# Three small parameter loads moved to the wide stage, and the last two state-space groups squared in place behind their stores

## The chip, the cores and the metric

The kernel runs as one program on one core of a Trainium2 chip. The metric is the device time of one execution in microseconds. Five engines work side by side in a core: PE (TensorE, the matmuls; its weight loads are listed as PEld), DVE (VectorE), ACT (ScalarE), POOL (GpSimd) and SP (SyncE, which here only issues DMAs). Each engine runs its own list of instructions in order, and an instruction can wait for instructions of other engines and for the landing of DMAs. ACT issues DMAs too: all stores to device memory are issued from its list.

## The reference

One layer of a decoder trunk on a sequence of 1024 tokens with 1024 channels, all in float32:

```python
mod = silu(c) @ ada_w + ada_b;  shift, scale, gate = split(mod, 3)
h = rms_norm(x, norm_w) * (1 + scale) + shift
gm_u, gm_v, gm_z, ssm_z, xbc, dt_raw, g_a, g_b = split(h @ w_in)
y_a = spatial_gating(gelu(gm_u), gelu(gm_v), ...) * silu(gm_z)
xs, bm, cm = split(silu(causal_conv(xbc, conv_w, conv_b)))
dt = softplus(dt_raw + dt_bias);  a = -exp(a_log)
y_b = ssd_scan(xs, dt, a, bm, cm) + xs * d_skip        # 8 groups of 4 heads
y_b = rms_norm per group of (y_b * silu(ssm_z)), times ssm_norm_w
merged = sigmoid(g_a) * (y_a @ w_proj_a) + sigmoid(g_b) * (y_b @ w_proj_b)
out = rms_norm(x + gate * (merged @ w_out), final_norm_w)
```

The three vectors `dt_bias`, `a_log` and `d_skip` have 32 numbers each. For the norm of `y_b` each group needs, per token, the sum of the squares of its 256 channels.

## The kernel before

The program is one long body that writes each engine's list in the order of the code; helpers marked `pin` keep their place, and other instructions may be moved by the scheduler. `load` (line 90) issues on SP, `store` (line 93) on ACT. PE is kept fed through the whole program, and everything else is arranged around its list.

**Early stage.** The modulation `mod` is a row times the matrix `ada_w`, taken in eight steps `n`. In each step PE computes a `matvec(n)` (16 matmuls `pm<-aw`, where `aw` holds half a megabyte of `ada_w`), ACT copies the result to a row (line 262), PE turns it into columns (`pm<-ones,row`), DVE makes the scale and the shift from it (`md`, lines 275 and 276), and ACT applies them to the transposed tokens (line 300: `b11h`, `hf` and others). With these, PE multiplies the first columns of `w_in`, `w0` (`acc<-b11h,w0h` and the like, line 81, the line of the helper that records every ordinary matmul). The weights of step `n + 2` are loaded in step `n`. In step 1, behind the loads of `aw` and `w0r` for step 3, SP also loads the three small vectors, each broadcast to all 128 partitions: `dtb`, `abc` and `dsk` (30.0 us into the program). DVE copies `dsk` into the narrower tile `dskt` (line 503); `dskt` is first read by the state-space stage.

**Wide stage.** From about 100 us on PE multiplies with weights whose blocks (`av`) SP loads and ACT and DVE split in two parts (`p2v0h`, `p2v0l`: a value and its remainder). The function `small_parameters` runs here; it loads the other small vectors (`pkb`), behind the last `av` loads.

**State-space stage** (about 930 to 1156 us). The eight groups are taken in four pairs, and each pair in four steps `s` of 256 tokens, the two groups in turn. A group's state `st` goes round from step to step: PE reads it (`yn<-sl,st`), POOL multiplies it by a decay (line 1157), DVE adds the new part `sp` from PE (line 1159), and PE reads it again. Between these, PE fills its time with the projection of `y_a` (`pma`, 3 x 8 x 8 pairs of matmuls, one pair for each half of the tokens), which `draw(n)` takes from a generator, `n` items at a time; `left[0]` counts what is left. The result of a pair of steps, `yz` (two tiles of 128 x 512), is stored to `yb_d` (line 93) and squared, so that PE can sum the squares over the channels (`pq<-ones`, in `post2`) and DVE and POOL make the norm's factors of it (`ssq`, lines 1221 and 1225). For the groups 0 to 5, and the first half of groups 6 and 7, the squares are written over `yz`, some steps after the store, and wait for it to land (line 1210). The second half of the groups 6 and 7 is the last of the stage: its squares go into two other tiles `sq`, taken from the rings `ea_r` and `ym_r` or `y1_r`, right behind the store (line 1205). The ring slot matters, because the stage behind it takes its tiles from the same slots.

**Projection of y_b** (from 1156 us). The normed `y_b` is multiplied with `w_proj_b` in 56 units: eight for each of the products `p1`, `p3`, `p6`, `p5`, `p7`, `p2`, `p4`, 12 matmuls each (line 1592). For a unit of `p1`, `loads` fetches a piece of `y_b` (`yn<-yb_d`), the factors `rb<-rs_d` for each second unit, and the weights `p1r`; `operands` normalises the piece (`y_norm`, line 1530 on DVE), and splits it (`p1bh` on ACT, `p1bl` on DVE) and the weights (`p1a` on ACT and on DVE). Six units are loaded ahead (`LOAD`) and four prepared ahead. The code of the first six comes behind the `post2` of groups 6 and 7, which comes when five items of `pma` are left.

Of the kernel before, what the change touches and what calls it, by code (L numbers as in the profile page):

```python
# [8 lines left out]
F32 = mybir.dt.float32  # L9
# [7 lines left out]
P = 128  # L17
# [4 lines left out]
NG = 8  # L22
# [13 lines left out]
def hybrid_kernel(  # L36
# [52 lines left out]
    def load(dst, src):  # L89
        pin(nc.sync.dma_start(dst, src))  # L90
# [81 lines left out]
    with tc.tile_pool(name="p0", bufs=1, reuse_waits="tile") as p0:  # L172
# [278 lines left out]
        for n in range(1, KT):  # L451
            todo = prepare(n + 1) if n + 1 < KT else {}
            for at, _ in enumerate(first_products(n), 1):
                if at == 1 and n + 2 < KT:
                    load_aw(n + 2)
                    load_w0(n + 2)
                if at == 1 and n == 1:
                    load(dtb, dt_bias.to_broadcast([P, NH]))
                    load(abc, a_log.to_broadcast([P, NH]))
                    load(dsk, d_skip.to_broadcast([P, NH]))  # L460
                if at in todo:
                    todo[at]()
                if at == 2 and n < KT - 1:
                    split_w0(n + 1)
                between(n, at)
# [17 lines left out]

    def small_parameters():

        pkb = wide("pkb").rearrange("p (i q) -> p i q", q=P)
        G.memset(pkb[:, 0], 0.0)
        at = 0
        for src, n in [(conv_b, 32), (ssm_norm_w, 16), (gm_ln_w, 8), (gm_ln_b, 8)]:
            load(pkb[at : at + n, 0], src[0].rearrange("(r q) -> r q", q=P))  # L490
            at += n
        load(pkb[:, 1], conv_w[0].rearrange("k (i q) -> (k i) q", q=P))
        later(4, small_parameters2, pkb)
# [580 lines left out]
    class Group:  # L1074
# [118 lines left out]
        def post(self, q):  # L1193
# [6 lines left out]
                later(5, self.squares, yz, [yz[:, j] for j in range(2)])  # L1200
                later(17, self.post2, q, [yz[:, 0]])
            else:
                self.late = sq = [turn(r, f"sq{g}", F32) for r in (ea_r, (ym_r, y1_r)[g % 2])]
                for j in range(2):
                    pin(A.activation(sq[j], yz[:, j], AF.Square))
                G.tensor_add(sq[0], sq[0], sq[1])

        def squares(self, yz, sq):
            for j in range(2):
# [264 lines left out]
        run_tasks()  # L1474


    draw(left[0] - 5)
    for late in groups[NG - 2 :]:
        late.post2(1, late.late[:1])
    room.extend(ea_r[0] + [st_r[0][1]])  # L1480
    room.extend(tag for k in range(KT - 2) for tag in ya_tags[k])

# [200 lines left out]
    def ahead(u):  # L1683
        if u + LOAD < len(units):
            loads(u + LOAD)
        if u + LEAD < len(units):
            operands(u + LEAD)

    for u in range(LOAD):
        loads(u)  # L1690
        if u > 1:
            operands(u - 2)
    draw(left[0] + 1)
    room.extend(tag for k in (KT - 2, KT - 1) for tag in ya_tags[k])
    for tags, _ in (war_r[0], wah_r[0], wal_r[0], tha_r):
# [235 lines left out]
```

## Time and profile before

| | |
|---|---|
| median of 3 runs | 1400.12 us (1399.7 to 1400.92) |
| the profiled execution | 1404.41 us |
| its span, from the first instruction to the last | 1402.7 us |
| mean granted TensorE clock | 0.993 |
| busy: DVE, ACT, POOL | 74%, 57%, 13% of the span |
| DMA | 288.60 MB, mean 206 GB/s |

A row of the timeline gives an instruction, or several alike behind each other: its start in microseconds of the span, its length, engine, line, operation, the tile written and the tiles read, the shape, the count (x16), and in brackets how long the engine had been idle before it and what it was waiting for. A row with SPq or ACTq is the issue of a DMA. A row of the windows gives a stretch of time, then for each engine its busy time and the number of instructions, and at the end the granted clock of PE (1.00 is full, 0.50 half), the busy share of the DMA engines and the bytes that they moved per second.

### The profile page before, as it was taken

How to read it: one execution, taken by the hardware profiler on the slowest of the kernel's cores; microseconds unless marked ns; L12 is line 12 of the kernel's file. 1: busy time of each engine (PE TensorE's matmuls, PEld its weight loads, DVE VectorE, ACT ScalarE, POOL GpSimd, SP SyncE). 2: the span in 40 equal slices, each digit the busy share in tenths (PEclk: the TensorE clock that was granted, in tenths of full speed). 3: DMA queues.
4: the chain of work that ended last, by engine and by line, in shares of the span. 5: the costliest groups of instructions: out<-in, count | busy, mean ns of one | idle time of the engine just before them, and what ended most of it. 6: DMA issues, size and time to landing. Idle time of an engine off the chain costs nothing.

```text
span 1402.7 us, 20203 instructions
## 1 busy us (share of the span) xinstructions
PE 1370.8 (98%) x6951; PEld 1133.6 (81%) x6951; DVE 1041.7 (74%) x1724; ACT 800.0 (57%) x1447; POOL 189.1 (13%) x191
## 2 busy tenths in 40 slices
PE   8999999999999999999999999999999999999997
PEld 6588888888888888888888888888888877788786
DVE  4685876777778789788888885398777736859976
ACT  4664666667556566465576555677666714233443
POOL 1000000000000000000000000038868760000002
PEclk9999999999999999999999999999999999999999
DMA  8674534343435667787675764698787719978913
GB/s 265 176 234 137 151 120 121 100 126 118 130 99 148 195 196 246 229 260 210 196 218 177 234 205 139 212 362 305 270 272 266 266 65 323 346 250 298 381 63 120
DMA packets 247228, 288.60 MB, mean 206 GB/s; under 512 B 14509, under 2 KB 194133, under 8 KB 247125
## 3 DMA queue, kind: packets, MB, share of 16 engines
q1 hardware_dynamic: 173716, 203.76, 45.5%
q10 hardware_dynamic: 73408, 83.54, 17.5%
q8 instruction: 55, 0.90, 0.3%
q14 instruction: 49, 0.39, 0.1%
HBM read 199.79 MB, written 87.46 MB: 205 GB/s over the span
## 4 chain that ended last, share of the span: by engine, by line
PE 69%; DMA 11%; DVE 8%; ACT 4%; issue 3%; SPq 2%; POOL 2%; ACTq 0%; DVEq 0%; POOLq 0%
PE xz L565 6%; PE xx L565 6%; PE xg L565 5%; PE xcb L565 5%; PE xuz L565 5%; PE pma L81 3%; PE vx L954 3%; PE yx L565 3%; PE yz L565 3%; PE ycb L565 3%; PE yg L565 3%; PE ox L1775 2%; PE yuz L565 2%; SPq L90 2%; DMA yn<-yb_d 2%
## 5 line engine op out<-in xcount | busy, mean ns | idle before, releaser
L1104 POOL TENSOR_SCALAR_AFFINE_SELECT dcy<-dcy 128x1024 f32<-128x1024 f32 x32 | 35.0, 1092 | 794.6 <-DMA yl<-ya_d 748.6
L1109 ACT ACTIVATE dcy<-dcy,nacs 128x128 f32<-128x128 f32 x256 | 78.5, 388 | 14.1 <-POOL dcy L1104 13.7
L1101 ACT ACTIVATE ea<-dcy 64x512 f32<-64x512 f32 x64 | 40.1, 626 | 13.0 <-DMA dcy<-acs_d 12.5
L1189 DVE TENSOR_TENSOR ym<-yn,ea 128x512 f32<-128x512 f32 (+1 forms) x32 | 19.9, 622 | 32.8 <-PE yn L81 32.8
L81 PE MATMUL pma<-yh,wah 128*128 128x512 f32 x128 | 43.9, 424 | 0.0
L1129 DVE TENSOR_TENSOR dcy<-dcy,pc 128x1024 f32<-128x1024 f32 x32 | 38.9, 1217 | 5.0 <-PE pc L84 4.0
L81 PE MATMUL pma<-yh,wal 128*128 128x512 f32 x128 | 42.6, 414 | 0.0
L1024 ACT ACTIVATE ac<-ac 128x1024 f32<-128x1024 f32 x32 | 34.0, 1061 | 13.5 <-DVE ac L1022 13.2
L1191 POOL TENSOR_TENSOR yz<-y,sl 128x512 f32<-128x512 f32 x32 | 41.4, 1293 | 0.9
L81 PE MATMUL pma<-yl,wah 128*128 128x512 f32 x128 | 40.3, 396 | 0.0
L1530 DVE SCALAR_TENSOR_TENSOR yn<-yn,par,rb 128x512 f32<-128x512 f32 x32 | 23.8, 747 | 21.7 <-DMA yn<-yb_d 21.7
L1190 POOL TENSOR_TENSOR y<-y,ym 128x512 f32<-128x512 f32 (+1 forms) x32 | 36.5, 1142 | 14.6 <-DVE ym L1189 14.6
L81 PEld LDWEIGHTS yn<-sl,st 128*128 128x128 f32 x224 | 30.2, 191 | 8.4 <-POOL yz L1211 2.5
L81 PE MATMUL sp<-xe,bn 128*128 128x256 f32 x112 | 33.7, 418 | 3.1 <-DVE ssq L1221 1.6
L81 PE MATMUL yi<-dcy,xd 128*64 128x128 f32 x512 | 35.9, 284 | 0.7 <-DVE st L1159 0.7
L81 PE MATMUL yn<-sl,st 128*128 128x128 f32 x224 | 31.1, 276 | 5.2 <-DVE st L1159 5.2
L1790 POOL TENSOR_TENSOR r<-r,fnw 128x512 f32<-128x512 f32 x4 | 5.3, 1334 | 228.6 <-ACT junk L1788 228.6
L1022 DVE SCALAR_TENSOR_TENSOR ac<-c2x,cwt,ac 128x1023 f32<-128x1023 f32 (+2 forms) x24 | 30.7, 1280 | 6.2 <-ACT ac L1020 6.1
L1022 DVE SCALAR_TENSOR_TENSOR ac<-c2cb,cwt,ac 128x1023 f32<-128x1023 f32 (+2 forms) x24 | 30.6, 1275 | 5.6 <-ACT ac L1020 5.5
L824 ACT CAST wbb<-wbr 128x512 fp32r<-128x512 f32 x32 | 19.8, 619 | 26.1 <-DMA wb_d<-wbb 20.5
L986 ACT ACTIVATE vm<-vm,vr 128x128 f32<-128x128 f32 x64 | 25.8, 484 | 14.9 <-DMA vm<-v_d 10.3
L1157 POOL TENSOR_TENSOR st<-st,cd 128x256 f32<-128x256 f32 x48 | 32.9, 685 | 9.7 <-PE yn L81 6.3
(2974 smaller groups left out, 4385.3 us busy)
## 6 DMA issues: line engine op xcount, KB each, us to landing
sl<-s_d SPq DMA_DIRECT2D x32, 768.0 KB
s_d<-ac ACTq DMA_DIRECT2D x32, 512.0 KB
wb_d<-wbb ACTq DMA_DIRECT2D x32, 512.0 KB
dcy<-acs_d SPq DMA_DIRECT2D x32, 512.0 KB
av<-in_w_in_dram SPq DMA_DIRECT2D x36, 256.0 KB
aw<-in_ada_w_dram SPq DMA_DIRECT2D x16, 512.0 KB
wbr<-in_w_proj_b_dram SPq DMA_DIRECT2D x32, 256.0 KB
yb_d<-yz ACTq DMA_DIRECT2D x32, 256.0 KB
```

The costliest lines, as they stand in the source:

```text
L81: pin(PE.matmul(acc, l, r, start=first, stop=last))
L565: pin(PE.matmul(ps, lw[:, k * P : (k + 1) * P], r[k], start=first and n + k == 0, stop=n == 2 and k == 3, skip_group_check=not first))
L954: pin(PE.matmul(ps[pn][j], l[:, j * P : (j + 1) * P], r, start=nm in ("p1", "p5", "p2") and n + units[i][1] == 0, stop=n == 2 and k == 3, ...
L1022: V.scalar_tensor_tensor(ac[:, s:], cc[:, : S - s], conv_wt[:, 3 - s, i : i + 1], ac[:, s:], op0=ALU.mult, op1=ALU.add)
L1024: A.activation(ac, ac, AF.Silu)
L1101: A.activation(ea[hh * HD : (hh + 1) * HD], dcy.rearrange("p (j e) i l -> p e j (i l)", e=2)[hh * HD : (hh + 1) * HD, hh], AF.Exp)
L1104: G.affine_select(out=d8, in_=d8, compare_op=ALU.is_ge, fill=-1e30, base=0, pattern=[[0, 2 * HPG], [1, P]], channel_multiplier=-1)
L1109: A.activation(dcy[:, h, i, :], dcy[:, h, i, :], AF.Exp, bias=sub[:, i, h : h + 1])
L1129: V.tensor_tensor(d3, d3, pc[:, 0:256].unsqueeze(1).to_broadcast([P, HPG, 256]), op=ALU.mult)
L1157: G.tensor_mul(v3(s2), v3(self.st), fac(cd, g, s)[:, i].unsqueeze(2).to_broadcast([P, HPG, HD]))
L1190: G.tensor_add(y1[:, :, t0:], y1[:, :, t0:], m[:, :, t0:])
L1191: G.tensor_mul(yz, y1, sl[:, 4:6])
```

## The change

The loads of `dtb`, `abc` and `dsk` go from step 1 of the early stage to the head of `small_parameters`, ahead of its other loads. The second halves of groups 6 and 7 are squared in place, as the others are, as a task five steps behind the store (`late_squares`); the tiles `sq` are gone. The two calls of `post2` are taken apart: group 6's comes with eight items of `pma` left, ahead of the code that loads the first units of the projection of `y_b`; group 7's comes with three items left, inside that code, behind the loads of unit 3 and the operands of unit 1.

```diff
@@ early stage, step n, behind the first product
                 if at == 1 and n + 2 < KT:
                     load_aw(n + 2)
                     load_w0(n + 2)
-                if at == 1 and n == 1:
-                    load(dtb, dt_bias.to_broadcast([P, NH]))
-                    load(abc, a_log.to_broadcast([P, NH]))
-                    load(dsk, d_skip.to_broadcast([P, NH]))
                 if at in todo:
                     todo[at]()
...
     def small_parameters():
 
+        load(dtb, dt_bias.to_broadcast([P, NH]))
+        load(abc, a_log.to_broadcast([P, NH]))
+        load(dsk, d_skip.to_broadcast([P, NH]))
         pkb = wide("pkb").rearrange("p (i q) -> p i q", q=P)
...
@@ Group.post
             else:
-                self.late = sq = [turn(r, f"sq{g}", F32) for r in (ea_r, (ym_r, y1_r)[g % 2])]
-                for j in range(2):
-                    pin(A.activation(sq[j], yz[:, j], AF.Square))
-                G.tensor_add(sq[0], sq[0], sq[1])
+                self.late = [yz[:, j] for j in range(2)]
+                later(5, self.late_squares)
+
+        def late_squares(self):
+            sq = self.late
+            for j in range(2):
+                pin(A.activation(sq[j], sq[j], AF.Square))
+            G.tensor_add(sq[0], sq[0], sq[1])
...
-    draw(left[0] - 5)
-    for late in groups[NG - 2 :]:
-        late.post2(1, late.late[:1])
     room.extend(ea_r[0] + [st_r[0][1]])
...
+    draw(left[0] - 8)
+    groups[6].post2(1, groups[6].late[:1])
     for u in range(LOAD):
         loads(u)
         if u > 1:
             operands(u - 2)
+        if u == 3:
+            draw(left[0] - 3)
+            groups[7].post2(1, groups[7].late[:1])
     draw(left[0] + 1)
```

**DVE in the early stage, before.** The rows are in the order of DVE's list; `b22l` and `b11l` are remainders of the tokens for the first product, `md` the modulation of step 2.

```order
L304 TENSOR_TENSOR b21l_198<-hf_434,b21h_194 128x512
L223 TENSOR_TENSOR w0l_347<-w0r_345,w0h_346 128x256
L304 TENSOR_TENSOR b22l_182<-hf_434,b22h_178 128x512
L503 COPY dskt<-dsk 64x16 x2
L275 TENSOR_TENSOR md_497<-pm_466,par 128x1
L276 TENSOR_SCALAR md_497<-pm_466,par 128x1
L304 TENSOR_TENSOR b11l_159<-hf_500,b11h_155 128x512
```

**The same place with the change, and then the place in the wide stage to which the copy goes**, about 100 rows further down in DVE's list. (The same lines of code have other numbers with the change: 1 lower here and in the groups, 3 higher from `late_squares` to the end of the state-space stage.)

```order
L304 TENSOR_TENSOR b21l_198<-hf_434,b21h_194 128x512
L223 TENSOR_TENSOR w0l_347<-w0r_345,w0h_346 128x256
L304 TENSOR_TENSOR b22l_182<-hf_434,b22h_178 128x512
L275 TENSOR_TENSOR md_494<-pm_463,par 128x1
L276 TENSOR_SCALAR md_494<-pm_463,par 128x1
L304 TENSOR_TENSOR b11l_159<-hf_497,b11h_155 128x512
```

```order
L884 TENSOR_TENSOR p7v2l<-av_2_1163,p7v2h 128x512
L884 TENSOR_TENSOR p7v3l<-av_3_1190,p7v3h 128x512
L884 TENSOR_TENSOR p2v0l<-av_0_1209,p2v0h 128x512
L502 COPY dskt<-dsk 64x16 x2
L884 TENSOR_TENSOR p2v1l<-av_1_1211,p2v1h 128x512
L884 TENSOR_TENSOR p2v2l<-av_2_1230,p2v2h 128x512
```

The copy of `dsk` no longer stands ahead of `md`; it stands between two splits of the wide stage, `p2v0l` and `p2v1l`.

**DVE at the last step of group 6** (`s` = 3), before and then with the change; `xe` and `xd` are inputs of group 7's step 3, `y` the direct part of group 6's result, `st` the state that PE's next `yn` reads.

```order
L1129 TENSOR_TENSOR dcy_3_10556<-dcy_3_10556,pc_3_10795 128x1024
L1125 TENSOR_TENSOR xd_3_10804<-px_3_10794,dthq 128x512
L1125 TENSOR_TENSOR xe_3_10806<-px_3_10794,dde 128x512
L1185 TENSOR_SCALAR y_3_10838<-sl_3_10483,dskt,yi_3_10811 128x256 x2
L1159 TENSOR_TENSOR st_3_0_10822<-st_3_0_10822,sp_3_10820 128x256
```

```order
L1128 TENSOR_TENSOR dcy_3_10556<-dcy_3_10556,pc_3_10795 128x1024
L1124 TENSOR_TENSOR xd_3_10804<-px_3_10794,dthq 128x512
L1124 TENSOR_TENSOR xe_3_10806<-px_3_10794,dde 128x512
L1530 TENSOR_SCALAR yn_0_10964<-yn_0_10964,par_139,rb_0_10962 128x512
L1184 TENSOR_SCALAR y_3_10838<-sl_3_10483,dskt,yi_3_10811 128x256 x2
L1158 TENSOR_TENSOR st_3_0_10822<-st_3_0_10822,sp_3_10820 128x256
```

The `y_norm` of unit 0 of the projection of `y_b`, which stood behind the last `ssq`, stands here inside the last step of group 6, ahead of `y` and `st`.

**ACT from the last stores of groups 6 and 7 to the first operands of the projection**, before and then with the change. `yb_d_95` and `yb_d_96` are the two stores of group 6, `yb_d_97` and `yb_d_98` those of group 7.

```order
L93 DMA yb_d_95<-yz_2_10705 128x512
L93 DMA yb_d_96<-yz_2_10705 128x512
L1205 ACTIVATE sq_10847<-yz_2_10705 128x512
L1205 ACTIVATE sq_10848<-yz_2_10705 128x512
L1422 DMA mt_d_81<-tha_0_10596 128x512
L1422 DMA mt_d_81<-tha_1_10599 128x512
L93 DMA rs_d_63<-tri 8x128
L93 DMA yb_d_97<-yz_2_10786 128x512
L93 DMA yb_d_98<-yz_2_10786 128x512
L1205 ACTIVATE sq_10894<-yz_2_10786 128x512
L1205 ACTIVATE sq_10895<-yz_2_10786 128x512
L1567 COPY p1bh_10999<-yn_0_10981 128x512
```

```order
L93 DMA yb_d_95<-yz_2_10705 128x512
L93 DMA yb_d_96<-yz_2_10705 128x512
L1425 DMA mt_d_81<-tha_0_10596 128x512
L1425 DMA mt_d_81<-tha_1_10599 128x512
L93 DMA rs_d_63<-tri 8x128
L93 DMA yb_d_97<-yz_2_10786 128x512
L93 DMA yb_d_98<-yz_2_10786 128x512
L1208 ACTIVATE yz_2_10705<-yz_2_10705 128x512 x2
L1208 ACTIVATE yz_2_10786<-yz_2_10786 128x512 x2
L1567 COPY p1bh_10982<-yn_0_10964 128x512
L1572 COPY p1a_10966<-p1r_10967 128x512
```

Group 6's squares moved from behind its own store to behind group 7's, and all four squares now read and write the stored tile; the first operand copies of the projection still stand behind them. On SP the three small loads moved, and nothing else; PE's list differs in the places of the two `pq` alone. SP's list has the loads of the projection in the same order as before, but the first of them, `rb`, takes a ring slot that group 6's `sq` held before until its `pq`, and that now has been free since `ea` was last read there, in the groups' third step.

## The prediction

> **What bounds the kernel now.** The first view is part 1 of the page, the busy time of the engines.
>
> ```profile
> PE 1370.8 (98%) x6951; PEld 1133.6 (81%) x6951; DVE 1041.7 (74%) x1724; ACT 800.0 (57%) x1447; POOL 189.1 (13%) x191
> ```
>
> PE is busy for 98% of the span, so the time falls only where PE stands still or works at a lower clock. The second view is the list of PE's waits (total, times, longest).
>
> ```profile
> PE x0p L1592 <- ACT p1a L1572: 4.6, 1, 4.6
> ...
> PE acc L81 <- ACT b11h L300: 2.6, 1, 2.6
> ```
>
> The longest wait is before the projection of y_b, and another of the longest is in the early stage. The change touches what leads to both. I call them place A (early) and place B.
>
> **Place A: what the small loads hold up.** The timeline has the chain: SP, DVE, ACT, then PE, and in front the matmul that `md` needs.
>
> ```profile
> 30.50 0.43 SPq L90 DMA_DIRECT2D dsk<-in_d_skip_dram  x1
> ```
> ```profile
> 32.14 0.50 PE L81 MATMUL pm<-ones,row 128*128 128x1 f32 x4
> ```
> ```profile
> 36.28 0.35 DVE L503 COPY dskt<-dsk 64x16 f32<-64x16 f32 x2 [4.35 <-DMA dsk<-in_d_skip_dram]
> ```
> ```profile
> 37.03 0.78 ACT L300 ACTIVATE b11h<-px,md 128x512 fp32r<-128x512 f32 x1 [5.56 <-DVE md L276]
> ```
> ```profile
> 37.86 0.73 PE L81 MATMUL acc<-b11h,w0h 128*128 128x512 f32 x2 [2.60 <-ACT b11h L300]
> ```
>
> DVE waits 4.35 us for a tiny load that lands 5.4 us after its issue ended (36.28 less 30.93). The `md` behind it could have run from 32.64, when PE's `pm` ended. Without the copy `b11h` runs at about 33.0 and is ready at 33.8, and PE comes for it at 35.26 (37.86 less 2.60). So the gap goes, with 1.4 us to spare, and PE's earlier rows don't change.
>
> The gap has a second price, seen in the windows (clock is the number behind POOL's).
>
> ```profile
> 38.60:42.00 3.40, 3.40 (x22) 2.08 (x23) 3.16 (x6) 2.41 (x5) 0.00 (x0) 0.50 0.12 33
> ```
>
> Behind the gap PE works 3.4 us at about half clock, 1.7 us of work lost. To size both prices in one, I compare the starts of alternate matvecs, which enclose like work (each pair of steps holds one `pd<-hf,wd`).
>
> ```profile
> 29.66 1.07 PE L81 MATMUL pm<-aw,scz 128*32 128x256 f32 x16
> ```
> ```profile
> 45.32 1.07 PE L81 MATMUL pm<-aw,scz 128*32 128x256 f32 x16
> ...
> 57.22 1.07 PE L81 MATMUL pm<-aw,scz 128*32 128x256 f32 x16
> ```
>
> From 29.66 to 45.32 are 15.66 us, from 45.32 to 57.22 are 11.90: 3.8 us lost. Counted directly it is 2.6 of gap and 1.7 of half clock, 4.3. I take **4.0**; the bounds are 2.6 (a low clock that comes anyway) and 4.3.
>
> **Where the three loads go.** SP now issues them behind the last `av`, and the copy stands on DVE before `p2v1l`.
>
> ```profile
> 99.34 8.12 SPq L90 DMA_DIRECT2D av<-in_w_in_dram  x8
> ```
> ```profile
> 111.85 0.69 DVE L885 TENSOR_TENSOR p2v1l<-av,p2v1h 128x512 fp32r<-128x512 f32 x1 [2.03 <-ACT p2v1h L884]
> ```
> ```profile
> 130.68 0.39 PE L954 MATMUL vz<-p2v1l,b21h 128*128 128x512 f32 x1
> ```
>
> Issued from 107.5 to 108.9 at 0.43 each, and landing 5.4 us later, they hold DVE to some 114.3, 2.5 us past its due time. PE uses `p2v1l` at 130.68, so 16 us of slack lie behind it: **0**. If that cover were gone it would cost those 2.5.
>
> **Place B: the loads of the projection.** SP's waits (the DMA queue's own), then the timeline.
>
> ```profile
> SPq L90 <- PE pq L81: 38.0, 1, 38.0
> ```
> ```profile
> 1152.67 0.32 SPq L90 DMA_DIRECT2D rb<-rs_d  x1
> 1153.08 0.38 SPq L90 DMA_DIRECT2D yn<-yb_d  x1
> ```
> ```profile
> 1158.44 0.75 DVE L1530 SCALAR_TENSOR_TENSOR yn<-yn,par,rb 128x512 f32<-128x512 f32 x1 [4.75 <-DMA yn<-yb_d]
> ```
> ```profile
> 1159.30 0.62 ACT L1567 CAST p1bh<-yn 128x512 fp32r<-128x512 f32 x1 [11.88 <-DVE yn L1530]
> ```
> ```profile
> 1155.30 0.63 PE L81 MATMUL pma<-yh,wal 128*128 128x512 f32 x2
> 1160.49 0.80 PE L1592 MATMUL x0p<-p1bh,p1a 128*128 128x512 f32 x1 [4.56 <-ACT p1a L1572]
> ...
> 1165.64 0.39 PE L1592 MATMUL x0p<-p1bh,p1a 128*128 128x512 f32 x1
> ...
> 1168.41 0.47 PE L1592 MATMUL x0p<-p1bh,p1a 128*128 128x512 f32 x1
> ```
> ```profile
> 1162.00:1164.00 2.00, 2.00 (x5) 1.54 (x6) 2.00 (x4) 0.43 (x1) 0.00 (x0) 0.50 1.07 384
> ```
>
> SP stands 38 us, because `rb` takes the slot of group 6's `sq` and must wait for its `pq`. Everything for unit 0 then comes in a row, and PE, done at 1155.93, waits 4.56 us. Its first unit takes 5.15 us (1160.49 to 1165.64) at clock 0.50, the next 2.77: 2.4 more. Together **7.0** to be had.
>
> With the change `rb`'s slot is free by the third step, and SP's `yn` for unit 0 goes out at about 1130.6, when its own slot falls free with a `yn` of PE and this `st` of POOL:
>
> ```profile
> 1129.84 0.61 POOL L1157 TENSOR_TENSOR st<-st,cd 128x256 f32<-128x256 f32 x1 [1.35 <-PE yn L81]
> ```
>
> The rest follows in steps as slots fall free, from 1142 on.
>
> Three things take some of it back.
>
> First, `y_norm` of unit 0 now stands ahead of `st` on DVE.
>
> ```profile
> 1132.92 0.68 DVE L1125 TENSOR_TENSOR xe<-px,dde 128x512 f32<-128x512 f32 x1
> ...
> 1134.30 0.41 DVE L1159 TENSOR_TENSOR st<-st,sp 128x256 f32<-128x256 f32 x1
> ```
> ```profile
> 1134.72 1.05 PE L81 MATMUL yn<-sl,st 128*128 128x128 f32 x8
> ```
>
> PE reads that `st` the moment it is there (1134.71), so each delay of DVE is one of PE. Queued behind `y_norm` are `y`, `st` and `ym`. It costs 0.67 (0.75, overlapped) if the load has landed by 1133.5, 3 us after its issue; the row at 1158.44 has 5.4 for a load among many, which would make it 3.0. DMA is idle here, so I take **0.9**; bounds 0.6 and 3.0.
>
> Second, the squares wait for the stores. What a store takes to land, from ACT's rows of the stage:
>
> ```profile
> 1111.71 0.35 ACTq L93 DMA_DIRECT2D yb_d<-yz  x1
> ...
> 1112.09 0.46 ACTq L93 DMA_DIRECT2D yb_d<-yz  x1
> ...
> 1117.30 0.63 ACT L1210 ACTIVATE yz<-yz 128x512 f32<-128x512 f32 x1 [1.04 <-DMA yb_d<-yz]
> ...
> 1120.10 0.63 ACT L1210 ACTIVATE yz<-yz 128x512 f32<-128x512 f32 x1 [2.17 <-DMA yb_d<-yz]
> ...
> 1145.41 0.82 ACTq L93 DMA_DIRECT2D yb_d<-yz  x2
> ```
>
> From issue to square: 5.6 and 8.0 us, beside 1.75 MB of loads. Group 7's stores go out at 1145.41 and 1145.82. At 5.6 the last square runs at 1151.4, POOL's sum (1.29) ends at 1153.3, and PE comes to that `pq` at about 1153.5: no wait. Behind the squares on ACT stand `p1bh` and `p1a`, and behind these on DVE `p1bl` and the second part of `p1a`, about 3 us in all: ready at 1155, due at 1155.8. At 8.0 all is 2.4 later and PE waits 2.2. I take 5.6, since fewer loads run here, and **0.3**; bounds 0 and 2.2.
>
> The Trainium skill, "DMA: Bandwidth & Descriptors", section "Anatomy of one DMA — SWDGE (gpsimd) path", gives about 2.0 us fixed plus the bytes at 436 GB/s, for another path of issue. By it a 256 KB store would land in an estimated 2.6 us and this term be 0; the rows above, at more than twice that under load, decide.
>
> Third, unit 8, the first of `p3`. Its `p3bl` stood behind the `y_norm` of unit 10; now that of unit 11 stands ahead of it too.
>
> ```profile
> 1182.59 0.75 DVE L1530 SCALAR_TENSOR_TENSOR yn<-yn,par,rb 128x512 f32<-128x512 f32 x1 [2.68 <-DMA yn<-yb_d]
> 1183.25 0.68 DVE L1568 TENSOR_TENSOR p3bl<-yn,p3bh 128x512 fp32r<-128x512 f32 x1
> 1184.47 0.75 DVE L1530 SCALAR_TENSOR_TENSOR yn<-yn,par,rb 128x512 f32<-128x512 f32 x1 [0.53 <-DMA yn<-yb_d]
> ```
> ```profile
> 1184.79 0.39 PE L1592 MATMUL x3p<-p1bh,p1a 128*128 128x512 f32 x1
> ```
>
> PE ends `p1` at 1185.0. In these times `p3bl` would end at 1185.8 instead of 1183.9, 0.8 too late. The loads behind unit 8 come earlier by about as much as PE does, so I take **0.8**; bounds 0 and 2.
>
> All else in the moved code keeps its count: four squares at 0.63, two sums at 1.29 and 16 `pq` matmuls are the same before and after.
>
> **The sum.** 4.0 + 7.0 − 0.9 − 0.3 − 0.8 = 9.0 us. The profiled execution took 1404.41 (span 1402.7, 1.7 around it), 4.3 more than the median of the runs; 9.0 off it is 1395.4, and off the median 1400.12 it is **1391.1**, which is what I forecast.
>
> **The rivals.**
>
> *The wait moves to the stores.* If group 7's stores land after 8.0 us, PE waits 2.2 at `pq`, and may work at half clock behind it. For that, a wait of this size must lower the clock:
>
> ```profile
> 1124.45 2.04 PE L81 MATMUL sp<-xe,bn 128*128 128x256 f32 x4 [1.64 <-DVE ssq L1221]
> ```
> ```profile
> 1125.00:1126.00 1.00, 1.00 (x5) 0.80 (x3) 0.15 (x1) 0.00 (x0) 1.00 (x2) 0.50 0.00 0
> ```
>
> A wait of 1.64 us is followed by clock 0.50, for some 3.4 us of work as at A, so 1.7 lost. Price 2.2 + 1.7, less the 0.3 already in: 1394.7. For it speaks that five loads share the DMA with the stores; against it, that nothing else moves then.
>
> The Trainium skill, "TensorE: Matmul & The Clock Gate", section "Part 1: The HAM clock gate", puts the fall to half clock behind an idle window of about 3.4 us. By it waits of 1.64 and 2.60 would leave the clock whole, and this rival would be an estimated 1393.0. The trace disagrees with both rows (1.64 and 2.60 us, each followed by 0.50), so the price with the clock stands.
>
> *The load of unit 0 lands late in the groups' chain.* PE waits 2 to 3 us for `st`, with 1.7 of clock behind it: 2.8 to 3.8 more than forecast, about 1394.4. The idle DMA speaks against it.
>
> *Place B gains nothing,* because the `p3` stage behind it, with its loads and its DVE, starts no earlier: only A's 4.0, 1396.1. For it speak 384 GB/s in the window row above and that DVE waits there for `yn` again and again; against it, that those loads go out earlier as well.
>
> *Slower.* The `y_norm` within the groups' chain waits for a load that SP cannot issue at 1130.6, since a slot or an earlier DMA holds the queue, as it did for 38.0 us before. PE then stands for as long as the load is late, with clock 0.5 behind. A and B bring 11.0 less 1.1, so it decides from about 8 us of lateness (plus 1.7 of clock) on; at 12 it would be 1404. The freeing events at 1130.5 speak against it.
>
> *The change doesn't do what it says:* PE's gap at A was due to something else and B's loads still wait: 1400. Both chains are read step by step above, so little is left for it.
>
> **How the numbers follow.** Forecast 0.52 (its own range 1388.8 to 1393), stores 0.15, late load in the chain 0.12, B without gain 0.08, slower 0.08, nothing 0.05. The range runs from 1388.5 (4.3 + 7.0 and 0.6 taken back, with a small margin) to 1396.3, past the third rival. A measurement of this kernel can tell about 0.2%, 2.8 us: faster 0.87, within it 0.05, slower 0.08.
>
> **What would show it.** In A: no wait of PE for `b11h` and clock 1.00 from 36 to 42 us. In B: SP's `rb` long before 1152, `x0p` behind `pma` without a gap, first unit 2.8 us. Against me: a wait of PE for POOL's sum at the last `pq`, a wait for `st` over 1.5 us near 1130, a wait for `p3bl` over 1 us.

## The result, and the profile after

The changed kernel takes **1387.98 us** (median of 4 runs, 1385.46 to 1391.49), the kernel before in the same comparison 1400.52 (4 runs, 1399.7 to 1402.12). The ratio is 0.9911 with a 95% interval of 0.9887 to 0.9935: 12.5 us faster, between 9 and 16. The forecast was 1391.1, with a range that began at 1388.5; the time lies 0.5 us below it. The profiled execution took 1387.35 us with a span of 1385.6 (before: 1404.41 and 1402.7). One execution of `before_dve6` further down (1709.15 us at a mean granted clock of 0.751) ran in a slower state; it counts in that run's median and in none of the ratios.

Part 1 of the page, the busy time of the engines, now reads:

```profile
PE 1363.9 (98%) x6951; PEld 1131.5 (82%) x6951; DVE 1042.8 (75%) x1724; ACT 801.4 (58%) x1447; POOL 190.4 (14%) x191
```

The counts are those of before. PE's busy time fell by 6.9 us, though it does the same work: that work runs at full clock where it had run at about half. Some 1.7 of it, an estimate from 3.4 us at half clock, are no part of the change: in this profile of before the clock fell behind a wait for `ssq` at 1124, and in this one of after it didn't (see the last section). The rest of the gain is waits. Both long waits of before are gone from PE's list (total, times, longest):

```profile
PE yn L81 <- DVE st L1158: 4.7, 4, 2.2
...
PE sp L81 <- DVE ssq L1224: 1.6, 1, 1.6
...
PE oy L1780 <- DVE ma11h L1631: 0.3, 1, 0.3
```

**Place A.** The same alternate matvecs as before, from the timeline of PE, and then the windows where the clock had been 0.50:

```profile
28.98 1.07 PE L81 MATMUL pm<-aw,scz 128*32 128x256 f32 x16
...
40.47 1.07 PE L81 MATMUL pm<-aw,scz 128*32 128x256 f32 x16
...
52.47 1.07 PE L81 MATMUL pm<-aw,scz 128*32 128x256 f32 x16
```
```profile
36.00:40.00 4.00, 3.97 (x27) 3.19 (x24) 3.07 (x7) 2.22 (x5) 0.00 (x0) 1.00 0.71 209
40.00:44.00 4.00, 4.00 (x35) 2.64 (x34) 2.90 (x6) 3.88 (x8) 0.00 (x0) 1.00 0.63 175
```

The first pair of steps takes 11.49 us, the second 12.00: the 15.66 of before have become a pair like any other, and the clock is whole. Where the copy went, the view of the tile `dskt` shows that DVE now waits for the same load in the wide stage, and nobody waits for DVE there:

```profile
L502 DVE COPY dskt<-dsk x2: 167/169/171, 107.9 to 108.1; 64x16 f32<-64x16 f32 x2
its engine sat idle before it (us, times) until:
  DMA dsk<-in_d_skip_dram: 2.9, 1
```

**Place B.** SP's rows, then PE's around the first unit of `p1`, and the window of the stage:

```profile
1109.18 0.63 SPq L90 DMA_DIRECT2D rb<-rs_d  x1
1123.72 0.32 SPq L90 DMA_DIRECT2D yn<-yb_d  x1
```
```profile
1148.80 0.62 PE L81 MATMUL pma<-yh,wal 128*128 128x512 f32 x2
1149.26 0.40 PE L1592 MATMUL x0p<-p1bh,p1a 128*128 128x512 f32 x1
...
1152.00 0.39 PE L1592 MATMUL x0p<-p1bh,p1a 128*128 128x512 f32 x1
```
```profile
1150.00:1200.00 50.00, 50.00 (x223) 41.17 (x222) 37.85 (x62) 16.25 (x28) 2.01 (x1) 1.00 0.95 344
```

SP issues `rb` 39 us ahead of the last `pma`, and `x0p` follows that `pma` without a gap. The first unit takes 2.74 us (1152.00 less 1149.26) where it took 5.15, and PE stands for nothing in 50 us. What the other three terms of the forecast became is read further down, beside the experiments.

### The profile page after: what moved, and what is told of

The parts are those of the page before. It is cut to its first block, busy times and chain, and to the rows that moved or that the text cites. A ratio compares the mean times of both kernels' runs of the same rounds, so it can differ in the third digit from the quotient of the medians.

```text
span 1385.6 us, 20200 instructions
## 1 busy us (share of the span) xinstructions
PE 1363.9 (98%) x6951; PEld 1131.5 (82%) x6951; DVE 1042.8 (75%) x1724; ACT 801.4 (58%) x1447; POOL 190.4 (14%) x191
## 4 chain that ended last, share of the span: by engine, by line
PE 85%; DMA 6%; DVE 3%; ACT 2%; issue 2%; POOL 2%; SPq 1%; POOLq 0%; ACTq 0%; DVEq 0%
PE xz L564 6%; PE xx L564 6%; PE xcb L564 6%; PE xuz L564 6%; PE xg L564 5%; PE pma L81 4%; PE ox L1780 3%; PE ycb L564 3%; PE yp L1592 3%; PE yz L564 3%; PE vx L953 3%; PE yx L564 3%; PE yg L564 3%; PE yuz L564 3%; DMA yb_d<-yz 2%
```

## The experiments

Each run was timed against the kernel before, on the same chip as the run. A single stretch of PE's list says more than the total here, since each part of the change has its own place. The columns of the table are in microseconds, from one profiled execution each: "A" from the start of the second to the start of the last of the eight matvecs (the expectations below call it "from the first to the last"); "step" from the second last to the last `sp` of the state-space stage, the place where PE waits for `st`; "B" from the `pq` of group 7's first half (1146.16 before) to the start of unit 1 of `p1`, the second of its units; "p3, p6" from the first unit of `p3` to the first of `p5`; "last" from the first `oy`, the last product, to the end of the span.

| kernel | median | ratio, 95% interval | A | step | B | p3, p6 | last |
|---|---|---|---|---|---|---|---|
| before (first profile) | 1400.52 | | 38.95 | 4.50 | 19.48 | 44.86 | 74.90 |
| before_again | 1399.89 | 1.0008 (0.9995–1.0021) | 38.20 | 4.50 | 19.89 | 43.73 | 75.29 |
| loads_only | 1397.13 | 0.9985 (0.9971–1.0000) | 34.89 | 4.48 | 19.49 | 43.79 | 74.12 |
| copy_pinned | 1395.72 | 0.9971 (0.9959–0.9984) | 34.86 | 4.50 | 19.39 | 44.48 | 72.82 |
| before_plus8 | 1403.75 | 1.0024 (1.0011–1.0038) | 38.58 | 4.50 | 19.43 | 45.66 | 75.25 |
| before_dve6 | 1398.16 | 0.9979 (0.9966–0.9993) | 37.71 | 4.48 | 20.17 | 45.56 | 72.84 |
| apart_only | 1399.57 | 0.9992 (0.9978–1.0005) | 38.39 | 4.50 | 17.54 | 47.65 | 73.47 |
| inplace_only | 1391.48 | 0.9937 (0.9922–0.9952) | 37.11 | 4.92 | 14.35 | 43.52 | 74.99 |
| late_only | 1389.13 | 0.9934 (0.9914–0.9955) | 40.20 | 4.92 | 12.37 | 43.52 | 72.79 |
| after (first profile) | 1387.98 | 0.9911 (0.9887–0.9935) | 34.89 | 4.92 | 12.38 | 43.52 | 72.81 |
| after_again | 1387.07 | 0.9909 (0.9892–0.9926) | 34.88 | 4.93 | 12.38 | 43.52 | 72.85 |
| late_copy | 1386.71 | 0.9906 (0.9891–0.9921) | 34.86 | 4.93 | 12.38 | 43.52 | 72.86 |
| after_pinned | 1386.64 | 0.9903 (0.9888–0.9918) | 34.87 | 4.50 | 12.37 | 43.52 | 72.86 |
| after_dve3 | 1384.64 | 0.9900 (0.9872–0.9928) | 34.86 | 4.92 | 12.37 | 43.52 | 72.82 |

The stretch between A and B, 1077.6 to 1083.6 us long, scatters by 6 us with no tie to any part of the change. So the columns tell the parts apart, and the totals only bear them out.

### loads_only: only the three loads move

Before, with the first two hunks of the change and no others:

```diff
-                if at == 1 and n == 1:
-                    load(dtb, dt_bias.to_broadcast([P, NH]))
-                    load(abc, a_log.to_broadcast([P, NH]))
-                    load(dsk, d_skip.to_broadcast([P, NH]))
...
     def small_parameters():
+        load(dtb, dt_bias.to_broadcast([P, NH]))
+        load(abc, a_log.to_broadcast([P, NH]))
+        load(dsk, d_skip.to_broadcast([P, NH]))
```

> The kernel before with the three small loads moved alone. Theory of the steps: the gain of the change is the sum of what each wait gives back, read from the two traces; this part gives 4.1 us (matvec starts 4.06 earlier), so about 1396.4, with x0p still waiting some 4.6 us for p1a and the waits of the later stages (p6bl 0.6, wlt 1.4) as before. Theory of scatter: what went beyond the forecast came from half-clock stretches that set in in some executions only; this part then gives between 2.6 and 4.3 and the sum of the parts alone (with the next kernel) stays at about 9.

The run took 2.1 us less than before (interval 0 to 4). A fell to 34.89, as in the changed kernel, and the wait at B stays, as the row of PE's waits shows:

```profile
PE x0p L1591 <- ACT p1a L1571: 4.5, 1, 4.5
```

A is thus this part's alone, and it is worth 3.6 us on the table: 38.45 is the mean of the seven profiles with the copy at its old place, 34.87 that of the seven without.

### late_only: only the late part

Before, with all hunks but the first two (the squares in place as `late_squares`, the two `post2` apart and behind loads).

> The late part alone: squares in place behind the store, the two products of squares apart; the small loads stand where they stood before. Theory of the steps: 7.1 at x0p, less 0.5 for y_norm within the groups' chain, plus 1.3 at p3 to p6 and 1.4 at the last product, whose waits for DVE go because the loads of the projection are ahead: about 9.3 us, 1391. Theory of scatter: the waits behind x0p go or stay by chance, and the part gives 5 to 6.5 us, 1394 to 1395. The wait of PE for b11h (2.6 us) stays by both.

It took 9.2 us less (6 to 12). B is 12.37 and the early gap is whole, with its half clock in the windows behind it:

```profile
PE acc L81 <- ACT b11h L300: 2.6, 1, 2.6
```
```profile
36.00:42.00 6.00, 4.67 (x24) 2.65 (x25) 3.63 (x9) 3.98 (x7) 0.00 (x0) 0.56 0.32 91
```

The two parts add up within their intervals: 2.1 and 9.2 are 11.3, the whole change is worth 12.5 to 12.7.

### before_again and after_again: both kernels once more

No edit; the two were run with the two parts, on the same chip, so that all stretches have a second profile.

> The kernel before once more, for its profile: the first profiled execution took 1404.41 us, 4.3 over the median of its runs. Theory of the steps: the waits (b11h 2.6, x0p 4.6, p6bl 0.6, wlt 1.4) are there again within 0.3, and what differs is a half-clock stretch or two. Theory of scatter: the two small waits behind x0p are not there in each execution. Time by both: 1399.7 to 1402.

> The changed kernel once more: its four runs spread over 6 us (1385.46 to 1391.49). Theory of the steps: 1387 to 1389 again, ratio 0.991, and what sets the runs apart is a half-clock stretch behind one of the state-space stage's waits. Theory of scatter: the median comes nearer to 1391.

The ratios are 1.0008 and 0.9909, and most stretches repeat: B is 19.89 and 12.38, "step" 4.50 and 4.93. One doesn't: "p3, p6" of before was 44.86 and is 43.73, since the wait for `p6bl` (0.6 in the first profile) isn't there in the second; that is what the theory of scatter had said of it. What the second pair of profiles settled is that the column "last" is no scatter between the two kernels, 74.90 and 75.29 against 72.81 and 72.85, over 2 us that no term of the sum had. I come back to it under before_plus8.

### copy_pinned: the loads stay, the copy goes

Before, with DVE's copy held at the place where the code has it, in the wide stage. The loads are issued in the early stage as before.

```diff
-            V.tensor_copy(dskt[part, :], dsk.rearrange("p (i h) -> p i h", h=2)[part, :, hh])
+            pin(V.tensor_copy(dskt[part, :], dsk.rearrange("p (i h) -> p i h", h=2)[part, :, hh]))
```

> The kernel before with the small loads where they were; only DVE's copy of dsk is held at its place in the code, in the wide stage, so that it no longer stands ahead of md. Theory of the copy: the loads cost nothing by themselves, PE's gap of 2.6 us at b11h and the half clock go as with the loads moved, and from the first to the last matvec PE takes 34.9 us as there (38.2 to 40.2 in the runs with the copy in its old place): 2 to 4 us faster. Rival, that the issue and transfer of the three loads delays the loads of aw and w0 behind them: part of the gap stays, 36 us or more.

It is 4.1 us faster (2.2 to 5.7), and A is 34.86. Alternate matvecs, as before:

```profile
28.85 1.07 PE L81 MATMUL pm<-aw,scz 128*32 128x256 f32 x16
...
40.33 1.07 PE L81 MATMUL pm<-aw,scz 128*32 128x256 f32 x16
```

The pair of steps that took 15.66 us takes 11.5, as in the changed kernel. The scheduler had moved the copy from the wide stage up into the early one, and it is that copy, waiting on DVE ahead of `md`, that cost the time. The issue of the three loads on SP and their transfers cost nothing that A shows. The 4.1 us aren't A's alone: "last" is 72.82 here, for the reason found under before_plus8.

### late_copy: the late part and the pinned copy

The changed kernel with the loads back in the early stage and the copy pinned, so that only the copy's place is left of the first part.

> The late part of the change, the small loads at their old place, and DVE's copy of dsk held at its place in the wide stage. If the copy was all that the early loads cost, this is the changed kernel without its first hunk: 34.9 us from the first to the last matvec and 1386 to 1388. Rival: the loads at their old place still cost something beside the late part, 1389 or more.

It takes 1386.71, the changed kernel 1387.98 and 1387.07: nothing is missing. Moving the loads did its work by moving the copy.

### inplace_only: in place, the products not apart

Before, with `late_squares`, but both `post2` where they were, behind each other and ahead of the loads.

```diff
-                self.late = sq = [turn(r, f"sq{g}", F32) for r in (ea_r, (ym_r, y1_r)[g % 2])]
-                for j in range(2):
-                    pin(A.activation(sq[j], yz[:, j], AF.Square))
-                G.tensor_add(sq[0], sq[0], sq[1])
+                self.late = [yz[:, j] for j in range(2)]
+                later(5, self.late_squares)
...
```

(`late_squares` follows as in the change.)

> The kernel before with the squares of the last halves in place behind their stores, and both products still together with five items of pma left, ahead of the code of the loads. Theory of the slot: what held the loads of the projection was the ring slot of sq alone, so SP's first rb goes out 40 us earlier again and x0p starts without a gap; in the trace of the changed kernel the sum of group 7's squares was ready about when PE would come to its product with five items left, so PE waits 0 to 1 us there: 1389 to 1391, like the late part alone. Rival, that the products must stand apart: PE waits 2 us or more at the second product for the sum of the squares, and half clock behind it: 1393 to 1395.

The loads go out early, as in the changed kernel, and it is 8.7 us faster (6.7 to 10.9). But B is 14.35, 2.0 more than with the products apart. PE's row of the second `pq`, and the window behind it:

```profile
1148.29 1.05 PE L81 MATMUL pq<-ones,yz 128*128 128x1 f32 x8 [0.29 <-POOL yz L1210]
```
```profile
1150.00:1152.00 2.00, 2.00 (x7) 1.54 (x6) 2.00 (x7) 1.46 (x3) 1.20 (x1) 0.54 0.96 358
```

With both `pq` in a row, group 7's is reached before POOL's sum is there. The wait is only 0.29 us, yet the clock behind it is 0.54, and that is where most of the 2.0 goes. In before the same 16 matmuls stood in a row without a wait (from 1151.65 on), and the clock stayed at 1.00 from 1153 to 1156. This is the rival of the stores in small. Standing apart is worth 2.0 us, 0.3 of it the wait and the rest clock.

### apart_only: the products apart, not in place

Before, with only the two `post2` moved as in the change; `sq` still takes ring tiles.

> The kernel before with the two products apart (eight and three items left) and the squares in the ring slots as before. Theory of the slot: rb still waits for group 6's product, which now ends about 1.4 us earlier; the gap before x0p falls from 4.6 to some 3.2 us and the half clock behind it stays: 1397 to 1399. Rival, that the place of the products is what counts: 1392 to 1394.

No net change (1.1 us faster, 0.7 slower to 3.1 faster). SP's `rb`, and two rows of PE:

```profile
1146.32 0.32 SPq L90 DMA_DIRECT2D rb<-rs_d  x1
```
```profile
1153.97 0.60 PE L1589 MATMUL x0p<-p1bh,p1a 128*128 128x512 f32 x1 [3.00 <-ACT p1a L1569]
...
1191.54 0.62 PE L1589 MATMUL y0p<-p3bl,p3a 128*128 128x512 f32 x1 [2.15 <-DVE p3bl L1565]
```

`rb` still waits for the slot of group 6's `sq`, and goes out when that group's `pq` frees it, now with `pma` still to come (it was 1152.67 before). That shortens the gap at B only from 4.56 to 3.00. And what B gains, 2.1 (19.64, the mean of the six kernels without the late part, less 17.54), is lost again in `p3`: there PE waits 2.15 for `p3bl` and 47.65 stand against 44.68. So it is the squares in place that free the slot: alone they bring B from 19.64 to 14.35, 5.3 of the 7.3 us, and the products apart add the other 2.0 once the slot is free. And the third term of the forecast, a `p3bl` that comes too late, is a real mechanism; it bites here.

### after_pinned: the first y_norm held behind the groups' chain

The changed kernel with `y_norm` of unit 0 kept at its place in the code, so that DVE does `st` first.

```diff
-        V.scalar_tensor_tensor(t, t, snw[:, n : n + 1], rbs[n // 2, h], op0=ALU.mult, op1=ALU.mult)
+        keep = pin if (n, h) == (0, 0) else lambda i: i
+        keep(V.scalar_tensor_tensor(t, t, snw[:, n : n + 1], rbs[n // 2, h], op0=ALU.mult, op1=ALU.mult))
```

> The changed kernel with one instruction held at its place in the code: the y_norm of unit 0, which the scheduler had put ahead of y and st in group 6's last step, now stands behind group 6's last ssq. Theory of the steps: its 0.46 us on PE's path go, and the chain of unit 0 (y_norm, p1bh, p1bl, the second part of p1a) is ready about 1 us later than before, still ahead of PE; x0p without a gap: 0.4 us faster than the changed kernel in that stretch, too little for the clock on the wall. Rival, that the chain is too late then: a wait at x0p of 1 us or more and half clock behind it, 2 to 3 us slower than the changed kernel. DVE's list is 4 places longer ahead of the products of the last units; for that see the next run.

"Step" falls from 4.92 to 4.50 and nothing else moves; the difference in time to after_again (0.9903 against 0.9909) is inside the intervals. In the changed kernel DVE's rows are

```profile
1126.53 0.74 DVE L1530 SCALAR_TENSOR_TENSOR yn<-yn,par,rb 128x512 f32<-128x512 f32 x1
...
1127.97 0.41 DVE L1158 TENSOR_TENSOR st<-st,sp 128x256 f32<-128x256 f32 x1
```

and PE's row for that `st` is

```profile
1128.53 0.68 PE L81 MATMUL yn<-sl,st 128*128 128x128 f32 x4 [0.19 <-DVE st L1158]
```

The load of unit 0, issued at 1123.72, was there when DVE came at 1126.53, without a wait, so the term is `y_norm` alone: 0.42 us.

### before_plus8 and before_dve6: what makes the last part shorter

The column "last" fell by over 2 us in the changed kernel, behind work that the change doesn't touch. The waits of PE from 1300 on name the tile in before; in after only the 0.3 for `ma11h` is left (the row stands in its list above):

```profile
PE oy L1775 <- DVE wlt L1672: 1.4, 1, 1.4
PE oy L1775 <- DVE ma11h L1631: 0.5, 1, 0.5
```

`wlt` is prepared by DVE, and DVE was late from the stage of `p7` and `p2` on, because loads for it landed late; this link is read from the rows. SP's rows there, in before and then in after, show one issue of 2.29 us, and the like one of 0.43:

```profile
1256.67 2.29 SPq L90 DMA_DIRECT2D yn<-yb_d  x1
```
```profile
1241.60 0.43 SPq L90 DMA_DIRECT2D yn<-yb_d  x1
```

And beside it, in the view of the DMA queues over 5 us (packets, MB, share of 16 engines), stands one packet of the queue that carries instructions, first in before (1255 to 1260), then in after (1240 to 1245):

```profile
q14 instruction: 1, 0.01, 2.6%
```
```profile
q14 instruction: 1, 0.01, 0.4%
```

2.6% of 16 engines over 5 us are 2.1 us of one engine; 0.4% are 0.3. The same small packet took seven times as long in before, and SP's issue stood beside it for as long. My first thought, that loads and DVE run further ahead in the changed kernel, fell with these rows: at the start of `p7` DVE and SP stand alike to PE in both. The next was that the place of SP's list decides. To shift it, before_plus8 is the kernel before with eight more tiny loads in the wide stage, into a spare row of device memory that nothing reads:

```diff
+    spare_d = dt_([1, NH], "spare_d")
...
+        for _ in range(8):
+            load(spare_d, a_log)
```

> The kernel before with eight more DMAs of 128 bytes in the wide stage, into a spare row of device memory, where SP stands idle; they do nothing but move every later instruction of SP some 14 places down its list. In the three traces without the late part, SP's issue of yn or p2r 5.0 to 5.5 us behind the start of p7 took 2.0 to 2.7 us while a packet of the code queue ran, and PE waited 1.0 to 1.9 us for wlt behind it; in the three with it neither is there. Theory of the code's place: the stall comes where SP's list crosses into code that is not yet loaded, so with the list moved the stall moves into one of SP's waits and the wait for wlt is under 0.5: 1.3 to 2 us faster than before. Rival, that the stall comes from what the late part does to slots or DMAs: it is there again at 5 us behind p7, and the time is that of before.

This missed: the stall stayed ("last" 75.25), so SP's list does not decide. The eight loads cost time of their own (3.6 us by the medians, 1.5 to 5.3 by the interval). The profile has a wait of 2.7 us for ACT's `vc` in the wide stage that none of the others has; that the loads cause it was not tried. Tabulated by DVE's list instead, the packet shows an order. "Place" is the number of the first `y_norm` of `p2` in DVE's list, "comes" the time of the packet behind the start of `p7`, "length" its time on a DMA engine:

| kernels | place | comes (us) | length (us) | last (us) |
|---|---|---|---|---|
| late_copy | 2242 | 8.05 | 0.30 | 72.86 |
| late_only, after, after_again | 2243 | 7.37–7.95 | 0.30–0.37 | 72.79–72.85 |
| copy_pinned | 2244 | 6.88 | 0.32 | 72.82 |
| inplace_only | 2244 | 5.01 | 1.90 | 74.99 |
| before, before_again, loads_only, apart_only | 2245 | 5.01–5.21 | 1.55–2.58 | 73.47–75.29 |
| before_plus8 | 2245 | 4.98 | 1.66 | 75.25 |
| after_dve3 | 2246 | 3.17 | 0.54 | 72.82 |
| after_pinned | 2247 | 3.16 | 0.53 | 72.86 |
| before_dve6 | 2251 | 2.71 | 0.32 | 72.84 |

The further on that `y_norm` stands in DVE's list, the earlier the packet comes, though not by equal steps: it follows DVE's list. Slow it is only where it comes 4.98 to 5.21 us behind the start of `p7`. The test is before_dve6, the kernel before with six more small instructions at the very start of DVE's list, which write the same constant again:

```diff
-    V.memset(nhalf, -0.5)
+    for _ in range(7):
+        V.memset(nhalf, -0.5)
```

> The kernel before with six more such writes at the start of DVE's list. Theory of the code's place on DVE: the packet comes 3 to 4 us earlier, while SP waits for DVE and issues nothing, so it stops nobody; the last part takes 72.8 us in place of 74.9 and 75.3, and the kernel is 2 us faster. Rival, that without the late part SP stalls there in any case: 74 to 75.3 us again and the time of before.

As expected, the stall is gone without any part of the change: SP's issue takes 0.38 again, and PE's waits from 1300 on are those of the changed kernel.

```profile
1253.03 0.38 SPq L90 DMA_DIRECT2D yn<-yb_d  x1
```
```profile
PE oy L1776 <- DVE ma11h L1632: 0.3, 1, 0.3
```

Six idle instructions made the kernel 2.9 us faster (1.0 to 4.8).

### after_dve3: the stall put back

The changed kernel with three more of the same instructions, to bring its DVE list to a place at which the stall had been.

```diff
-    V.memset(nhalf, -0.5)
+    for _ in range(4):
+        V.memset(nhalf, -0.5)
```

> The changed kernel with three more writes of a constant at the very start of DVE's list (0.07 us each, beside the start of the loads); they move all later instructions of DVE 3 places down its list. In six profiles of kernels whose DVE list has the first y_norm of p2 at its place 2244 or 2245, a packet of the code queue 5 us behind the start of p7 took 1.6 to 2.6 us, SP's issue stood still beside it, and the last part of the program took 73.5 to 75.3 us; in four with it at 2243 (one: 2244) the packet came at 6 to 7 us, took 0.3, and the last part took 72.8. Theory of the code's place on DVE: at 2246 the slow packet and the stall at 5 us are there, and the last part takes 74 to 75.3: 1389 to 1390. Rival, that the late part itself removes the stall: 72.8 again, 1387.

This missed. The list stands at 2246 and the packet came at 3.17 us, ahead of the slow place, not at 5: "last" is 72.82. That DVE's list moves the packet is borne out, three places and it comes over four microseconds earlier. That one can place the stall by counting is not, since it isn't the count alone: inplace_only and copy_pinned share a count and differ by 1.9 us and by the stall. So before_dve6 shows that the stall can go without the change; that the changed kernel with the stall put back would be slower isn't shown.

## Why the prediction was right and where it was wrong

- **A, 4.0: right.** 3.6 on the table, within the bounds of 2.6 and 4.3, by the chain that was read (the copy ahead of `md`), as copy_pinned shows. That its new place costs nothing also held: DVE waited there 2.9 us and no other engine for it.
- **B, 7.0: right.** 19.64 to 12.38, 7.3 us, gap and half clock as split. It comes from the freed slot, as inplace_only and apart_only show; 2.0 of it need the products apart as well.
- **y_norm of unit 0, −0.9: half of it.** 0.42 in each kernel with the late part but the pinned one. The load landed in less than 2.8 us, where the forecast had added a bit for a load that takes longer.
- **The stores, −0.3: nothing, by the mechanism assumed.** The rows of ACT for group 6 and 7, and PE's second `pq`:

```profile
1137.67 0.85 ACTq L93 DMA_DIRECT2D yb_d<-yz  x2
...
1142.69 0.63 ACT L1208 ACTIVATE yz<-yz 128x512 f32<-128x512 f32 x1 [2.97 <-DMA yb_d<-yz]
1144.02 0.63 ACT L1208 ACTIVATE yz<-yz 128x512 f32<-128x512 f32 x1 [0.70 <-DMA yb_d<-yz]
1144.56 0.60 ACT L1567 CAST p1bh<-yn 128x512 fp32r<-128x512 f32 x1
```
```profile
1146.97 0.95 PE L81 MATMUL pq<-ones,yz 128*128 128x1 f32 x8
```

The two stores landed 5.0 and, from 1138.1, 5.9 us after their issue, about the 5.6 assumed. POOL's sum was there for PE, with no wait, and the casts behind the squares were done ahead of `x0p`.

- **Unit 8, the first of `p3`, −0.8: a step that failed.** It said that `p3bl` would come 0.8 too late, with "bounds 0 and 2", on the ground that "the loads behind unit 8 come earlier by about as much as PE does". In the changed kernel they come earlier by more. DVE's rows, then PE's use:

```profile
1165.98 0.75 DVE L1530 SCALAR_TENSOR_TENSOR yn<-yn,par,rb 128x512 f32<-128x512 f32 x1 [1.99 <-DMA yn<-yb_d]
1167.76 0.75 DVE L1530 SCALAR_TENSOR_TENSOR yn<-yn,par,rb 128x512 f32<-128x512 f32 x1 [1.03 <-DMA yn<-yb_d]
1168.43 1.29 DVE L1568 TENSOR_TENSOR p3bl<-yn,p3bh 128x512 fp32r<-128x512 f32 x2
```
```profile
1171.57 0.39 PE L1592 MATMUL y0p<-p3bl,p3a 128*128 128x512 f32 x1
```

The order on DVE is the one foreseen, two `y_norm` and then `p3bl`; but the first of these two `p3bl` ends near 1169.1, over 2 us before PE needs it. The reason stands one step ahead of it. SP's `yn` for the next units waits for two stores of `mt_d`, in before (ACT, then SP) and in after (ACT, then SP):

```profile
1168.01 0.92 ACTq L1422 DMA_DIRECT2D mt_d<-tha  x2
```
```profile
1172.78 0.32 SPq L90 DMA_DIRECT2D yn<-yb_d  x1
```
```profile
1154.39 0.92 ACTq L1425 DMA_DIRECT2D mt_d<-tha  x2
```
```profile
1156.43 0.32 SPq L90 DMA_DIRECT2D yn<-yb_d  x1
```

From the stores' issue to that `yn` are 4.77 us before and 2.04 after. In before SP's loads for the first units had gone out in one burst from 1153.08 on, with the last 0.9 us ahead of the stores; with the change they begin at 1123.72, and the last goes out 3.4 us ahead of the stores. The windows between the stores and that `yn`, of before and of after, have the DMA share and the GB/s at their end:

```profile
1168.00:1172.78 4.78, 4.78 (x24) 3.73 (x23) 4.78 (x8) 2.39 (x4) 0.00 (x0) 1.00 0.82 277
```
```profile
1154.40:1156.40 2.00, 2.00 (x11) 1.57 (x10) 2.00 (x4) 1.04 (x2) 0.00 (x0) 1.00 0.59 222
```

All fourteen profiles agree: from the stores' issue to that `yn` are 2.04 or 2.05 us in the seven with the squares in place, where SP issues five loads in the 8 us ahead of the stores, and 4.51 to 6.11 in the seven without, where it issues nine. That the fuller DMA is the reason for the longer landing is read from these rows, not tried by itself. What PE lost there in the first profile of before is a wait for `p6bl` and delays too short for this list:

```profile
PE x0p L1592 <- DVE p6bl L1568: 0.6, 1, 0.6
```

The stretch of `p3` and `p6` is 43.52 us in each of the seven profiles with the squares in place. In the six others with the products in their old order it is 43.73 to 45.66, 44.68 on average: **+1.2 instead of −0.8**, and only 0.2 and 0.3 in the two fastest of the six, before_again and loads_only, though their stores took 5.3 us. So how much of the late landing reaches PE varies, and why stays open. The late `p3bl` is a real wait, as apart_only shows with 2.15 us, in the one run where the loads still come in a burst and the products stand apart.

- **The last part, 2.3: the other step that failed, and the larger.** It was put at nothing. 75.1 (both profiles of before) became 72.8. It doesn't come from what the change does: with the change DVE's list up to there is two places shorter, so that the packet of instructions comes at another moment, and before_dve6 has the same gain without the change, while inplace_only, whose loads go out as early, keeps the stall (74.99). By these runs it is luck for the change. "All else in the moved code keeps its count" was true, and was taken to mean that all else keeps its time.

In sum, by the traces: 3.6 + 7.3 − 0.4 + 1.2 + 2.3 = 14.0. The comparison of runs has 12.5, between 9 and 16; the stretch between A and B scatters by more than the difference. The range's low end was 4.3 + 7.0 with 0.6 taken back, which rests on two terms being the only gains. It had no place for a stage further on to gain too, and the two that did, 3.5 us in all, are why the time lies below it. That it lies outside by 0.5 us and not inside is less than the four runs scatter; the two steps are wrong either way.

Of the rivals, the wait for the stores is seen only in inplace_only, where it is small and the clock is its price. The late load in the groups' chain, the slower case and the case of no gain at B have no trace of them in any run with the whole change.

## What to carry to other kernels

A wait that a scheduler made can be moved by holding one instruction in its place, and a slot can be freed by doing a thing in place: look for what stands in front of the waiting instruction in its engine's list, not for what it loads. Where loads that came in a burst are spread, look at the stores that shared the burst, and at the stage behind: that is where a forecast that stops at the removed wait falls short. A stretch that the change doesn't touch can still move, here by 2.3 us with the place of DVE's list, so a gain there needs a run of its own before the change gets the credit. And stretches between fixed instructions, over several profiles, tell parts of a microsecond apart that whole times, here with intervals of 3 us and more, don't.

## What the runs showed of the hardware that was not expected

**A slow packet of instructions stood beside a slow issue of a load.** A packet of 8 KB on the queue of instructions took 0.3 to 0.5 us in eight of the profiles. In the other six it took 1.55 to 2.58, and SP's issue of a load beside it was 1.5 to 2.7 us long. At which moment the packet comes follows DVE's list: three idle instructions at its start moved it by over 4 us. What makes the packet slow at 5.0 to 5.2 us behind the start of `p7` and not at 3.2 or 6.9 stays open. So does whether it holds up SP or both are slowed by a third thing: before_again has an issue of 1.36 us at 1258.62 with no such packet beside it.

**The clock falls behind short waits, and not behind each.** The changed kernel's wait of 1.62 us for `ssq`, and the window behind it:

```profile
1118.90 1.10 PE L81 MATMUL sp<-xe,bn 128*128 128x256 f32 x4 [1.62 <-DVE ssq L1224]
```
```profile
1120.00:1122.00 2.00, 2.00 (x11) 1.60 (x10) 0.42 (x1) 0.00 (x0) 2.00 (x3) 1.00 0.00 0
```

The same wait in before_plus8:

```profile
1124.14 2.05 PE L82 MATMUL sp<-xe,bn 128*128 128x256 f32 x4 [1.40 <-DVE ssq L1224]
```
```profile
1126.00:1128.00 2.00, 2.00 (x7) 1.61 (x6) 0.42 (x1) 0.00 (x0) 2.00 (x3) 0.65 0.00 0
```

1.62 us leave the clock at 1.00; 1.40 us in the other kernel, at the same place of the program, bring it down. The kernel before had 1.64 and 0.50 there, and 1.35 without a fall in before_again. Over the fourteen profiles the clock fell behind this wait in four (1.40, 1.55, 1.64 and 1.91 us) and stayed whole in ten (1.20 to 1.67 us), so its length alone doesn't decide. A fall of 3.4 us at half clock costs an estimated 1.7 us, so this is some of the scatter between executions. The Trainium skill, "TensorE: Matmul & The Clock Gate", section "Part 1: The HAM clock gate", says that the window in which activity is counted runs freely, and that the moment of a transition depends on where in it the first matmul lands. The rows fit that if the same holds of where a wait falls; no run here tries it. Its length for the fall, about 3.4 us of idle time, does not fit: 1.40 us here, and 0.29 among sixteen one-column `pq` in inplace_only, were enough.
